# Attention shifts through one row matmul, the closing norm of a row tile spread over two pairs, and score banks for the Fourier stage's transposes and mapping

## The chip, the cores and the metric

The kernel runs on one core of a Trainium2 chip. The metric is device time in microseconds (us) for one execution, and lower is better. The kernel before takes 3379.32 us, the median of three runs (3378.93 to 3382.05).

## What is computed

One layer of an encoder over 4096 tokens and 16 prepended meta tokens, width 1024. The reference, cut to what matters:

```python
u = rmsnorm(h, norm_g)
f_in, f_gate, q, k, v, a_gate = split(u @ w_in)
f_out = (real(fftn(f_in, axes=(position, channel of its group))) @ w_fmix + b_fmix) * silu(f_gate)
q, k  = rope(rmsnorm(q, q_g)), rope(rmsnorm(k, k_g))     # 8 query heads, 2 kv heads of dim 64
a_out = softmax(q @ k.T * 64 ** -0.5) @ v * silu(a_gate)   # 4112 keys, no mask
h = rmsnorm(h + concat(f_out, a_out) @ w_out, final_g)
return h[:, 16:]
```

## The kernel before

Products are made in float16 with a high and a low part of an operand, three matmuls for one product. Phase A (to about 738 us in the trace) makes the projections and folds the input for the Fourier transform; q, k, v and both gates go to DRAM. Phase B does the Fourier transform's second half and the attention. The order of the work in phase B is written out by hand: each engine takes its instructions in the order in which the Python code issues them, SyncE (SP) issues all of phase B's DMAs in one queue, and an instruction that waits holds everything behind it on its engine.

**Pairs and steps.** Attention runs over 8 blocks of 512 queries, and in each over 4 pairs of heads: 32 pairs, numbered `i` from 0, `(b, p)` in the code. A pair has 66 steps `j`, 33 key tiles for each of its two heads. A step (`qk`, `pvm`) makes the scores of 512 queries against 128 keys in a score bank (L983, L984), has ScalarE (ACT) take the exponential into `pe` (L987), has GpSimd (POOL) or VectorE (DVE) make `rr`, the low part (L989), and four steps later multiplies both parts with V (L1004 to L1011). `on_dve` says which steps' `rr` DVE makes: two steps after each entry of the list `AT`. When a head's 33 tiles are done, ACT copies its accumulator (`tt`, L1015), DVE takes a reciprocal (L1017), and POOL makes four operations of it (`ob`, L1019 to L1022).

**Banks.** PSUM's eight banks are: two tiles of two banks each that are called `m`, two score banks `s`, one for the attention accumulator `o`, one for `pd`/`po`. A tile is taken in turn, and its next user waits for the last reader.

**The shift.** The exponential is taken of score minus the row's maximum, and the maximum must be known before the pair begins. So while pair `i` runs, `max_units(i+1)` makes the next pair's scores a first time in `m` tiles (L928, two groups at each entry of `AT`, 32 in all) and DVE takes their maxima (L929, `mx`). `meta` does so for the 16 meta tokens, 8 small matmuls for a pair (L936, L938). At step 58 `red` reduces and scales them (L943, L944, `nm`), at step 61 `fin` turns them with 8 matmuls (L951) into rows, and two ACT copies (L954) put these into rows 64 to 95 of `qB`. There they meet a constant 256 in K's second half, so that the second score matmul (L984) subtracts the shift.

**The output.** From block 1 on each pair also finishes one 128-row tile of the block before: `out_tr` at step `TR` = 8 turns 1024 mixed channels with eight transposes into an `m` tile (L1047), ACT and DVE split it (`mh` L1050, `ml` L1051), and 48 matmuls (L1064) at steps 13 to 36 and 41 to 64 make the output projection. `out_end` at step 2 of the next pair closes the tile: the sum of squares on ACT (L1079), eleven DVE operations of which ten are on 128x1 values (the root), and the scaling `yo` (L1083).

**The Fourier stage.** 18 units of 50 matmuls (L772, L775), each followed by `gather` (ACT), `trans` (four transposes into an `m` tile, L798, then `thl` on ACT, DVE and POOL) and `mix` (24 matmuls into an `m` tile, then `mo` on DVE, L838, and POOL, L840). `flist` holds them in order, and `f_step(n, heavy)` does up to `n` matmuls and `heavy` of the transposes or mappings. Before pair 0, where nothing but pair 0's maxima can run beside it (the start below), each round does two groups of maxima and `f_step(18, 1)`. In pairs 0 to 3 each step does `f_step(5, ...)`; then `wo_load` and `wo_prep` fetch and split the eight pieces of the output weights (L911, L915, L916) until step 258 of 264.

## Time and profile before

| | us |
|---|---|
| median of 3 runs | 3379.32 |
| profiled execution, its own time | 3381.74 |
| its span, first to last instruction | 3380.0 |
| PE busy (share of the span) | 3275.9 (97%) |
| DVE busy | 2369.8 (70%) |
| ACT busy | 1735.4 (51%) |
| POOL busy | 2223.6 (66%) |
| phase A, to the first unit's last Fourier matmul | 738 |
| start of phase B, to pair 0's first score | 85 |
| pairs 0 to 3 | 356 |
| pairs 4 to 31 and the tail | 2201 |

A matmul's recorded duration is longer than the time by which the next one can start, so a busy PE can still have short waits in it: the start-to-start distance of neighbours says how long a matmul holds the array. The execution's own time is 1.7 us more than its span.

### The profile page before, as it was taken

How to read it: one execution, taken by the hardware profiler on the slowest of the kernel's cores; microseconds unless marked ns; L12 is line 12 of the kernel's file. 1: busy time of each engine (PE TensorE's matmuls, PEld its weight loads, DVE VectorE, ACT ScalarE, POOL GpSimd, SP SyncE). 2: the span in 40 equal slices, each digit the busy share in tenths (PEclk: the TensorE clock that was granted, in tenths of full speed). 3: DMA queues.
4: the chain of work that ended last, by engine and by line, in shares of the span. 5: the costliest groups of instructions: out<-in, count | busy, mean ns of one | idle time of the engine just before them, and what ended most of it. 6: DMA issues, size and time to landing. Idle time of an engine off the chain costs nothing.

```text
span 3380.0 us, 79039 instructions
## 1 busy us (share of the span) xinstructions
PE 3275.9 (97%) x33333; PEld 1909.7 (56%) x33333; DVE 2369.8 (70%) x3250; ACT 1735.4 (51%) x3019; POOL 2223.6 (66%) x2131
## 2 busy tenths in 40 slices
PE   7999999988999999999999999999999999999998
PEld 4555555546666555555555555555555555555554
DVE  6766565537667877777777777777777777777764
ACT  5443443322555655555555555555555555555553
POOL 3655555323667877777777777777777777777762
PEclk9999999999999999999999999999999999999999
DMA  7444443437431120010001000100100010010001
GB/s 218 140 162 137 144 145 125 128 116 215 136 117 50 51 54 24 20 45 20 20 20 45 20 20 27 57 20 20 45 20 20 20 45 20 20 39 20 20 20 57
DMA packets 142330, 223.61 MB, mean 66 GB/s; under 512 B 30390, under 2 KB 85510, under 8 KB 137622
## 3 DMA queue, kind: packets, MB, share of 16 engines
q1 hardware_dynamic: 128150, 193.38, 18.5%
q10 hardware_dynamic: 13824, 25.17, 2.0%
q8 instruction: 261, 4.28, 0.5%
q14 instruction: 95, 0.78, 0.1%
HBM read 157.38 MB, written 61.14 MB: 65 GB/s over the span
## 4 chain that ended last, share of the span: by engine, by line
PE 67%; DVE 6%; issue 2%; ACT 1%; POOL 0%; ACTq 0%; POOLq 0%; DVEq 0%
PE s L983 12%; PE s L984 12%; PE o L1004 11%; PE po L1064 9%; PE m L928 7%; PE o L1011 7%; PE pd L775 2%; PE o L1009 2%; PE o L1007 2%; DVE mx L929 1%; DVE yo L1083 1%; PE m L1223 1%; PE m L1047 1%; DVE r1t L1097 1%; DVE rf L1098 1%
## 5 line engine op out<-in xcount | busy, mean ns | idle before, releaser
L989 POOL TENSOR_TENSOR rr<-pe 128x512 f16<-128x512 f32 (+1 forms) x1541 | 1634.4, 1075 | 629.5 <-ACT pe L987 623.8
L987 ACT ACTIVATE pe<-s 128x512 f32<-128x512 f32 (+1 forms) x2112 | 1259.4, 597 | 1038.6 <-PE s L984 1011.0
L929 DVE TENSOR_REDUCE mx<-m 128x2 f32<-128x1024 f32 x1024 | 1206.1, 1217 | 261.2 <-PE m L928 257.3
L1011 PE MATMUL o<-VV,rr 128*128 128x65 f16 x8448 | 974.7, 193 | 1.1 <-POOL rr L989 0.5
L1011 PEld LDWEIGHTS <-rr 128*128 128x128 f16 x8448 | 784.4, 98 | 186.3 <-issue 12.0
L1004 PE MATMUL o<-VV,pe 128*128 128x129 f16 x6336 | 842.1, 222 | 13.8 <-ACT tt L1015 10.9
L1004 PEld LDWEIGHTS <-pe 128*128 128x128 bf16 x6336 | 587.0, 97 | 390.5 <-issue 223.4
L983 PE MATMUL s<-qA,K 128*128 128x512 f16 (+1 forms) x2112 | 800.9, 379 | 0.7 <-ACT pe L987 0.7
L984 PE MATMUL s<-qB,K 128*128 128x512 f16 (+1 forms) x2112 | 800.6, 379 | 0.4 <-ACT qB L954 0.4
L989 DVE TENSOR_TENSOR rr<-pe 128x512 f16<-128x512 f32 x571 | 486.2, 852 | 222.9 <-ACT pe L987 219.9
L1007 PE MATMUL o<-VV,pe 128*128 128x65 f16 (+1 forms) x2112 | 411.0, 195 | 0.0
L1009 PE MATMUL o<-VV,pe 128*128 128x64 f16 (+1 forms) x2112 | 410.1, 194 | 0.0
L84 PE MATMUL ps<-wh,xh 128*128 128x512 f16 (+2 forms) x1032 | 366.0, 355 | 9.2 <-ACT xh L287 9.2
L85 PE MATMUL ps<-wl,xh 128*128 128x512 f16 (+2 forms) x1032 | 365.9, 355 | 4.7 <-DVE wl L270 4.7
L86 PE MATMUL ps<-wh,xl 128*128 128x512 f16 (+2 forms) x1032 | 366.1, 355 | 1.9 <-POOL xl L288 1.9
L928 PE MATMUL m<-K,qP 64*128 64x512 f16 x2048 | 320.4, 382 | 26.8 <-DMA bias<-bias 12.7
L928 PEld LDWEIGHTS <-qP 64*128 64x128 f16 x2048 | 66.3, 94 | 253.9 <-issue 246.0
L1009 PEld LDWEIGHTS <-pe 128*128 128x128 bf16 (+1 forms) x2112 | 208.7, 99 | 0.0
L983 PEld LDWEIGHTS <-K 128*128 128x128 f16 (+1 forms) x2112 | 202.9, 96 | 7.9 <-issue 1.1
L1007 PEld LDWEIGHTS <-pe 128*128 128x128 bf16 (+1 forms) x2112 | 206.2, 98 | 0.0
L984 PEld LDWEIGHTS <-K 128*128 128x128 f16 (+1 forms) x2112 | 204.7, 97 | 2.0 <-issue 1.9
L288 POOL TENSOR_TENSOR xl<-xt,xh 128x1024 f16<-128x1024 f32 (+1 forms) x33 | 68.7, 2082 | 155.6 <-ACT xh L287 155.5
(192 smaller groups left out, 3676.9 us busy)
## 6 DMA issues: line engine op xcount, KB each, us to landing
ct<-cd SPq DMA_DIRECT2D x16, 1088.0 KB
room<-x SPq DMA_DIRECT2D x32, 512.0 KB
xt<-xt SPq DMA_DIRECT2D x32, 512.0 KB
sg<-fx SPq DMA_DIRECT2D x16, 1024.0 KB
xr<-x SPq DMA_DIRECT2D x32, 512.0 KB
out<-yo SPq DMA_DIRECT2D x32, 512.0 KB
fg_d<-g ACTq DMA_DIRECT2D x32, 256.0 KB
ag_d<-g ACTq DMA_DIRECT2D x32, 256.0 KB
```

Of the source, the lines that this page charges most:

```text
L84: T.matmul(out, lh, rh, start=first, stop=False, skip_group_check=skip)
L86: T.matmul(out, ll, rh, start=False, stop=last, skip_group_check=skip)
L928: T.matmul(t[:, e], q[rs, s, p], K[kv][rs, 4 * c:4 * c + 4, 0], start=True, stop=True)
L929: V.tensor_reduce(mx[:, s, :, c], t, axis=AX.X, op=ALU.max)
L983: T.matmul(s[:n], K[kv][:, t, 0, :n], qa, start=True, stop=False)
L984: T.matmul(s[:n], K[kv][:, t, 1, :n], qb, start=False, stop=True)
L987: S.activation(pe[:n], s[:n], AF.Exp, scale=HD ** -0.5)
L989: eng.tensor_tensor(out=rr[:n], in0=pe[:n], in1=hi[:n], op=ALU.subtract)
L1004: T.matmul(o[:, c0:c0 + 129], hi[:n, cs], va, start=t == 0 and s == 0, stop=t == NT, skip_group_check=True)
L1007: T.matmul(o[:, c0:c0 + 65], hi[:n, cs], vh, start=False, stop=t == NT, skip_group_check=True)
L1009: T.matmul(o[:, c0:c0 + 64], hi[:n, cs], vl, start=False, stop=t == NT, skip_group_check=True)
L1011: T.matmul(o[:, c0:c0 + 65], rr[:n, cs], vh, start=False, stop=t == NT, skip_group_check=True)
```

## The change

It has five parts, beside an equal grouping of two DMAs (`runs`: the last six key tiles come with two loads instead of six).

1. **One row matmul.** `nm` becomes one 128x32 tile with the eight shifts of a row side by side. `fin`, now at step 63, is one matmul, and a new `put` at step 64, one DVE operation on 8 partitions with 1024 elements each, spreads the rows into `qB` through a mask cut from the identity. The 8 matmuls and both ACT copies go. K has eight rows of 256 in place of one. `red` moves to step 61.
2. **Meta once a block.** `meta` does all four pairs of a block at step `MT` = 60 of the pair before the block (32 small matmuls and two DVE operations); for block 0 it does two pairs at a time. The result is kept in `met`, already scaled, and `red` takes the minimum with it.
3. **The closing norm in steps.** `out_end` becomes `square` (ACT, step 62), `root` (ten DVE operations, step 65) and `scale` (`yo` and its DMA, step 13 of the next pair). `AT` has 16 entries and not 17, `TR` is 11, the output matmuls stand at steps 14 to 37 and 38 to 61, and `ml` is issued one step after its transposes.
4. **The start.** `trans` and `mix` take score banks instead of `m` tiles ahead of block 0; their DVE and POOL operations are held back (`behind`) and issued by `catch_up` after the next group of maxima. `qload(0)` and `fix_load` are issued ahead of `f_step(50, 0)`, `fix_prep` and the last key tiles after the first round; the last `f_step` does 25 matmuls and not 9.
5. **Block 0.** Each step does 3 Fourier matmuls and not 5, so that the last one stands at step 29 of pair 3 and not at step 38 of pair 2. `wo_prep` runs every fifth step from step 256 on, 6 of the 8 in pair 4, where the first output tile begins.

```diff
         for t in ksb:
             G.memset(t, 0.0)
-            G.memset(t[:, :, 1, 1, 0:1], 256.0)
+            G.memset(t[:, :, 1, 1, 0:8], 256.0)
...
-        def trans(u):
+        def trans(u, early):
             n, sk = (P, stk) if u < 16 else (64, stk8)
-            t = pm.tile([P, 2, 512], F32, tag="m", name="m")
-            ps = t[:, 0].rearrange("p (g c)->p g c", c=P)
+            if early:
+                ps = pq.tile([P, 512], F32, tag="s", name="s").rearrange("p (g c)->p g c", c=P)
+            else:
+                ps = pm.tile([P, 2, 512], F32, tag="m", name="m")[:, 0].rearrange("p (g c)->p g c", c=P)
...
             S.activation(th, ps[:, :, :n], AF.Copy)
-            V.tensor_tensor(out=tl, in0=ps[:, :, :n], in1=th, op=ALU.subtract)
             S.activation(thr, th[:, :, ::-1], AF.Copy)
-            G.tensor_copy(tlr, tl[:, :, ::-1])
+
+            def rest():
+                V.tensor_tensor(out=tl, in0=ps[:, :, :n], in1=th, op=ALU.subtract)
+                G.tensor_copy(tlr, tl[:, :, ::-1])
+
+            behind.append(rest)
...
             def red():
                 m = sm.tile([P, 4, 2], F32, tag="mm", name="mm")
                 V.tensor_reduce(m, mx, axis=AX.X, op=ALU.max)
-                V.tensor_scalar(out=n[:, :, :, 0], in0=m.rearrange("p s e->p e s"), scalar1=-1.0 / 256.0,
-                                scalar2=None, op0=ALU.mult)
+                V.scalar_tensor_tensor(out=n[:, 0:8].rearrange("p (e s)->p e s", s=4),
+                                       in0=m.rearrange("p s e->p e s"), scalar=-1.0 / 256.0,
+                                       in1=met[b][:, :, p], op0=ALU.mult, op1=ALU.min)
 
             def fin():
                 t = pm.tile([P, 2, 512], F32, tag="m", name="m")
-                for e in range(2):
-                    for s in range(4):
-                        T.matmul(t[64:96, e, s * P:(s + 1) * P], n[:, e, s], id16, start=s == 0, stop=True,
-                                 skip_group_check=s > 0)
-                for e in range(2):
-                    S.activation(qB[b % 2][64:96, :, 4 * e + p], t[64:96, e].rearrange("p (s c)->p s c", s=4),
-                                 AF.Copy)
+                T.matmul(t[64:96, 0, :P], n, id16, start=True, stop=True)
+                rowt.append(t)
+
+            def put():
+                t = rowt.pop()
+                V.tensor_tensor(
+                    out=qB[b % 2].rearrange("p s (e q) c->p e s q c", e=2)[64:72, :, :, p],
+                    in0=t[64:72, 0, :P].unsqueeze(1).unsqueeze(1).broadcast_to([8, 2, 4, P]),
+                    in1=id32[64:72, 64:72].rearrange("p (e s)->p e s", s=4).unsqueeze(3).broadcast_to([8, 2, 4, P]),
+                    op=ALU.mult)
...
-        AT = [0, 4, 8, 12, 15, 19, 22, 26, 29, 33, 36, 40, 43, 47, 50, 53, 56]
-        TR, O0, O1 = 8, 13, 41
+        AT = [0, 4, 8, 14, 18, 22, 26, 29, 33, 37, 41, 45, 48, 52, 55, 58]
+        MT, TR, O0, O1 = 60, 11, 14, 38
...
-            if g >= 6:
-                f_step(5, 1 if mid else 0)
+            catch_up()
+            if 6 <= g < 4 * 66:
+                f_step(3, 1 if mid else 0)
...
-                if j == 2 and prev:
-                    out_end(*prev)
-                    prev = None
+                if j == TR + 1 and b > 0:
+                    low()
+                if j == TR + 2 and prev:
+                    prev[2]()
+                if j == 62 and b > 0:
+                    prev = out_end(b - 1, p, halves[1])
+                    prev[0]()
+                if j == 65 and b > 0:
+                    prev[1]()
```

What ACT does from the end of one regular pair into the next (regular: a pair that also finishes an output tile). Before, from the shifts' two copies at step 61 on; `xr,ss` is the sum of squares, `tt` the head's accumulator, `mh` the output tile's high part:

```order
L954 ACTIVATE qB_7751<-m 32x4x128 x2
L987 ACTIVATE pe<-s 128x512 x3
L987 ACTIVATE pe<-s 16x512
L987 ACTIVATE pe<-s 128x512 x3
L1079 ACTIVATE xr,ss<-hh 128x1024
L987 ACTIVATE pe<-s 128x512
L1015 ACTIVATE tt<-o 128x452
L987 ACTIVATE pe<-s 128x512 x5
L1050 ACTIVATE mh<-m 128x1024
```

And now, from the sum of squares at step 62 on (ACT's exponentials are now at L1027, its other lines 40 to 42 further down than before):

```order
L1121 ACTIVATE xr,ss<-hh 128x1024
L1027 ACTIVATE pe<-s 128x512 x2
L1027 ACTIVATE pe<-s 16x512
L1027 ACTIVATE pe<-s 128x512 x4
L1055 ACTIVATE tt<-o 128x452
L1027 ACTIVATE pe<-s 128x512 x8
L1090 ACTIVATE mh<-m 128x1024
```

The copies into `qB` are gone, and the sum of squares stands four exponentials earlier, no longer between step 2's exponential and `tt`.

DVE in the same stretch, before, from the end of the root to the second key group after the transposes (`mx` are maxima of keys, `rc` the reciprocal):

```order
L1098 TENSOR_SCALAR rf<-r1t,rf 128x1
L1083 SCALAR_TENSOR_TENSOR yo<-hh,rf,fgb 128x1024
L1017 RECIPROCAL rc<-tt 128x4
L929 TENSOR_REDUCE mx<-m 128x2 x2
L989 TENSOR_TENSOR rr<-pe 128x512
L1051 TENSOR_TENSOR ml<-m,mh 128x1024
L929 TENSOR_REDUCE mx<-m 128x2
L989 TENSOR_TENSOR rr<-pe 128x512
```

And now, from the end of the root, which stands at step 65 of the pair before (the row ahead of its first one is `put`):

```order
L1146 TENSOR_SCALAR rf<-r1t,rf 128x1
L955 TENSOR_REDUCE mx<-m 128x2 x2
L1029 TENSOR_TENSOR rr<-pe 128x512
L1057 RECIPROCAL rc<-tt 128x4
L955 TENSOR_REDUCE mx<-m 128x2 x2
L1029 TENSOR_TENSOR rr<-pe 128x512
L955 TENSOR_REDUCE mx<-m 128x2 x2
L1029 TENSOR_TENSOR rr<-pe 128x512
L1092 TENSOR_TENSOR ml<-m,mh 128x1024
L1129 SCALAR_TENSOR_TENSOR yo<-hh,rf,fgb 128x1024
L955 TENSOR_REDUCE mx<-m 128x2 x2
```

The root has left the place between step 2's `rr` and step 4's maxima, and `yo` now comes after three pairs of maxima and `ml`.

SP's queue at the border of the phases, before (`k_d` is phase A's last store, `qP` the queries for pair 0's maxima, `ct` a unit's Fourier table, `fgu` a gate):

```order
L189 DMA k_d<-ko 128x512 x2
L828 DMA fgu<-fg_d 121x512
L828 DMA fgu<-fg_d 128x512
L105 DMA ct<-cd 128x4352
L707 DMA qP_7753<-q_d 64x4x512 x2
L744 DMA wst<-wst 128x1024
L745 DMA sgn<-sgn 128x2
L746 DMA bias<-bias 128x512
L118 DMA K_6590<-k_d 128x256 x6
```

And now:

```order
L189 DMA k_d<-ko 128x512 x2
L710 DMA qP_7753<-q_d 64x4x512 x2
L747 DMA wst<-wst 128x1024
L748 DMA sgn<-sgn 128x2
L749 DMA bias<-bias 128x512
L843 DMA fgu<-fg_d 121x512
L843 DMA fgu<-fg_d 128x512
L105 DMA ct<-cd 128x4352
```

`qP` and what `fix_prep` needs now stand ahead of the gate and the table.

## Prediction

> **What bounds the kernel now.** I read the page's engine shares first (PE 97%, no other over 70%), then the windows by stage. Columns: length, then busy time of PE, PEld, DVE, ACT and POOL, then PE's granted clock and DMA.

> ```profile
> 738.10:823.00 84.90, 59.36 (x544) 42.83 (x545) 53.88 (x56) 12.72 (x31) 19.90 (x15) 0.92 0.69 207
> 823.00:1104.90 281.90, 277.69 (x3246) 181.20 (x3246) 185.28 (x197) 146.00 (x271) 194.14 (x187) 0.99 0.35 108
> 1104.90:1178.90 74.00, 67.05 (x812) 38.39 (x810) 67.47 (x61) 46.92 (x78) 62.39 (x58) 1.00 0.16 51
> 1178.90:1254.30 75.40, 75.30 (x868) 42.92 (x866) 55.18 (x57) 42.37 (x72) 56.71 (x59) 1.00 0.17 43
> 1254.30:3256.40 2002.10, 1967.38 (x22418) 1118.98 (x22415) 1507.80 (x1768) 1125.20 (x1899) 1473.84 (x1483) 1.00 0.09 27
> ```

> These are the start, pairs 0 to 2, pair 3, pair 4, and pairs 5 to 30 (26 pairs of 77.0 us). PE is the bound in the pairs, with short holes; in the start it is idle for 25 of 85 us; in pair 3 DVE is busy for 67 of 74 us. Next the chain that ended last, at the seam of two regular pairs, and who PE waits for in pairs 5 to 30 (total, times, longest):

> ```profile
> 1954.10 1.50 DVE yo L1083
> 1955.70 1.12 DVE mx L929
> 1956.87 1.09 PE m L1047 x8
> PE m L1047 <- DVE mx L929: 21.3, 26, 0.8
> PE o L1004 <- ACT tt L1015: 9.9, 26, 0.4
> ```

> Once a pair the chain leaves PE: root and `yo` hold DVE, the maxima behind them are late, and the transposes of step 8 find no free `m` tile. That is 0.8 us of 77. The second hole, 0.4 us, is the wait for `tt`. Pair 4 is the control: it finishes an output tile, but no earlier tile's `out_end` falls into it, and it takes 75.4. So `out_end` in its old place costs 77.0 - 75.4 = 1.6 us a pair.

> **The seam (pairs 5 to 30).** `out_end` leaves step 2, so both holes go: -1.6 if nothing takes their place. *One row matmul:* eight take 0.62 us below, of which one alone lasts 0.22, so each further one costs (0.62 - 0.22)/7 = 0.057, and seven fewer are -0.4. *One event of maxima fewer:* the scores of steps 7 and 8 start 0.79 us apart, a bare step; a score matmul holds PE for 0.22. Into an event it takes 0.30 (1884.37 to 1884.67), and the event's four matmuls, which run in twos, take 0.54 and not 0.43: two changes of shape, -0.2.

> ```profile
> 1942.32 0.62 PE L951 MATMUL m<-id,nm 128*32 128x128 f16 x8
> L951 PE MATMUL m<-id,nm 128*32 128x128 f16 x216 | 16.7, 220 | 0.0
> 1877.72 0.38 PE L983 MATMUL s<-qA,K 128*128 128x512 f16 x1
> 1878.51 0.38 PE L983 MATMUL s<-qA,K 128*128 128x512 f16 x1
> 1884.15 0.38 PE L983 MATMUL s<-qA,K 128*128 128x512 f16 x1
> 1884.37 0.38 PE L984 MATMUL s<-qB,K 128*128 128x512 f16 x1
> 1884.67 0.60 PE L928 MATMUL m<-K,qP 64*128 64x512 f16 x4
> 1885.21 0.23 PE L1004 MATMUL o<-VV,pe 128*128 128x129 f16 x1
> ```

> *The other head's `tt`:* 52 heads end in these pairs and 26 waits are listed, so mid pair the wait stays under the view's limit of 0.15 us; now the maxima of step 37 stand there, -0.1. *Meta once a block:* the same 32 matmuls in one event of their own, at most +0.1 a pair. Sum so far -2.2.

> What comes in. (a) *The sum of squares at step 62.*

> ```profile
> 1873.19 0.60 ACT L987 ACTIVATE pe<-s 128x512 f32<-128x512 f32 x1 [0.19 <-PE s L984]
> 1873.69 1.05 ACT L1079 ACTIVATE xr<-hh 128x1024 f32<-128x1024 f32 x1
> 1874.73 0.59 ACT L987 ACTIVATE pe<-s 128x512 f32<-128x512 f32 x1
> 1874.86 0.15 DVE L1080 TENSOR_SCALAR ss<-ss 128x1 f32<-128x1 f32 x1 [0.19 <-ACT xr L1079]
> 1877.16 1.52 DVE L1083 SCALAR_TENSOR_TENSOR yo<-hh,rf,fgb 128x1024 f32<-128x1024 f32 x1
> ```

> It puts the next exponential 1.54 us behind the one ahead (1873.19 to 1874.73). There are two score banks, so step 65's scores wait for step 63's exponential. An exponential starts about 0.7 us after its step (two score matmuls and the hand-over), so step 63's ends 0.7 + 1.54 + 0.59 = 2.8 us after step 62's start. PE reaches step 65 after three bare steps and `fin`, 3 x 0.79 + 0.25 = 2.6: a new wait of 0.2 to 0.3. At step 2 the maxima of step 4 hid this; at 62 to 65 no output matmul and no maxima fill the steps. (b) *`put`.* Its nearest row is `ml`, also 1024 elements a partition from PSUM, 1.2 us:

> ```profile
> L1051 DVE TENSOR_TENSOR ml<-m,mh 128x1024 f16<-128x1024 f32 x26 | 31.8, 1224 | 1.3
> L929 DVE TENSOR_REDUCE mx<-m 128x2 f32<-128x1024 f32 x832 | 980.2, 1217 | 201.6 <-PE m L928 198.9
> L989 DVE TENSOR_TENSOR rr<-pe 128x512 f16<-128x512 f32 x442 | 371.0, 839 | 143.5 <-ACT pe L987 140.8
> ```

> The row matmul ends about 1.5 us after step 62's start, `put` at 2.8, and L984 of the next pair, its first reader, is due at 3.7: covered, with 0.9 us to spare. (c) *DVE from `put` to step 18:* `put` 1.2, root 2.3 (1874.86 to 1877.16), four pairs of maxima 9.7, four `rr` 3.4, `ml` 1.2, `yo` 1.5: 19.3 us. PE takes about 20.5 for it (20 steps of 0.79, five events at 0.6, eight transposes, five output matmuls). So DVE keeps up, by little, and each `m` tile is free just ahead of its user. (d) *POOL's four `ob` operations* at step 3 stand in front of step 4's `rr`.

> ```profile
> 1185.73 0.30 POOL L1021 TENSOR_TENSOR ob<-tt,ag 128x64 f32<-128x64 f32 x1
> 1186.68 8.92 POOL L989 TENSOR_TENSOR rr<-pe 128x512 f16<-128x512 f32 x8
> 1877.55 1.28 POOL L1021 TENSOR_TENSOR ob<-tt,ag 128x64 f32<-128x64 f32 x1
> ```

> In pair 4 that `rr` starts at 1186.68, 7.8 us after the pair (1178.90), and ends 8.92/8 = 1.1 later, at 8.9. Without transposes at step 8 PE wants it at 8 x 0.79 + 3 x 0.6 + 0.4 = 8.5; today the hole at step 8 covers it. I take +0.3, bounds 0 and 1.1 (one `rr`). Net -2.2 + 0.3 + 0.3 = -1.6 a pair, x 26 = -42 us; bounds -2.2 and -0.8 a pair (-57 and -21).

> The last three rows show one POOL operation at 0.30 beside maxima and at 1.28 beside `yo` (1877.16): the two engines delay each other. [...] It speaks against this change, which moves `yo` beside a row of waiting `rr`; rival B has the price.

> **The start.** Who PE waited for, the timeline, a window and a DMA size:

> ```profile
> PE m L928 <- DMA bias<-bias: 12.7, 1, 12.7
> PE m L928 <- DVE mo L838: 3.9, 5, 0.8
> PE m L951 <- DVE nm L944: 2.7, 1, 2.7
> PE m L928 <- DVE thl L801: 2.5, 5, 0.5
> PE m L798 <- issue: 2.5, 1, 2.5
> 738.55 1.28 SPq L707 DMA_DIRECT2D qP<-q_d  x2
> 750.00:755.00 5.00, 3.76 (x15) 1.73 (x16) 1.42 (x2) 0.40 (x1) 0.00 (x0) 0.50 0.61 136
> 752.78 2.82 PE L775 MATMUL pd<-acs,ct 128*128 128x264 f16 x12
> 767.84 1.51 PE L775 MATMUL pd<-acs,ct 128*128 128x264 f16 x12
> ct<-cd SPq DMA_DIRECT2D x16, 1088.0 KB
> ```

> The first maxima need `qP` (the first wait's label names a DMA of the same burst). It was issued at 738.55 behind a 1088 KB table and a gate of half that; at the start's 207 GB/s these are 8 us. With `qP` ahead I take 10 of the 12.7 (bounds 7 and 12.7). `fix_prep` still waits for its weights, now behind two maxima, and holds the third group's for about 3 us; the 2.5 us wait at the first transposes (L798) is the same wait in today's place, so nothing is counted. After the long wait the granted clock is 0.50, and twelve Fourier matmuls take 2.82 us against 1.51: 1.3 us more, of which I count none, since a wait of 3 us stays. [...]

> In the rounds, `trans` and `mix` no longer hold `m` tiles: 3.9 + 2.5 of waits, -6. `nm`'s 2.7 us go under 16 more matmuls (+1.7, taken from block 0). `put` in place of `fin`'s two copies: +0.5 to -0.5, 0. Sum -10 - 6 - 2.7 + 1.7 = -17; bounds -23 and -10 (if DVE, at 54 of 85 us, leads in the rounds and half the waits stay).

> **Block 0 and pair 4.** Pair 3 has no Fourier matmul and no output: pair 4's 75.4 less 48 output matmuls at 0.22 and transposes (1.1) is 64, and it took 74: 10 us of waiting for DVE, where `wo_prep` comes on top. Pairs 0 to 2 have 535 Fourier matmuls at 0.11 (1.51 us for twelve, less the overlap) and 12 units of 24 mapping matmuls at 0.057 and four transposes at 0.11: 80 us, and 3 x 64 = 192: 272 of 282, another 10. Spread at 3 a step, DVE has room (185 of 282 us). Of the 20 I leave 3 at pair 0's start and 4 where `wo_prep` now meets the first output tile, six of these in 28 steps:

> ```profile
> L916 DVE SCALAR_TENSOR_TENSOR wol<-wot,woh x8: 1225/1466/2014, 1096.7 to 1174.9; 128x1024 f16<-128x1024 f32 x8
> ```

> That is -13; the row matmul and the event, 0.6 in five pairs, -3; the 16 matmuls, -1.7. Sum -18; bounds -24 and -8 (`wo_prep` costs as much as today).

> **The end.** Pair 31's `tt` hole loses the sum of squares: -1.

> **Sum.** -42 - 17 - 18 - 1 = -78 us: the profiled execution from 3381.7 to 3304, the median of the runs, 2.4 below it, from 3379.3 to 3301.

> **Rivals.** *B: DVE and POOL become the bound at the seam.* `yo` shuts `rr` out for 1.5 us, DVE's 19.3 of 20.5 us turns into waits for `m` tiles, and half the seam's gain goes: 26 x 0.9 = +23, 3324. For it: the small margins in (c) and (d). Against: four steps between scores and their use. 0.2. *C: the start and block 0 give only their lower bounds* (-10, -8): +17, 3318. 0.08. *D: slower.* `red`, `fin`, `put`, L984 go from DVE to PE to DVE to PE within five steps at every seam. If `put` is over 0.9 us late, PE stands at step 0 with all scores behind it. The sum turns over where a seam loses 78/26 = 3.0 us more than forecast, `put` 3.9 late; at 4.5 us it is -78 + 117 = +39, 3418. Against: DVE has about 2 us of work in steps 59 to 63. 0.04. *E: no change,* 3379: every hole comes back as another. Against: pair 4 shows 75.4 without the hole. 0.02.

> **How the numbers follow.** The forecast has 0.66. All the bounds at once give -105 and -40; since they don't fall together I take 3276 to 3334, which holds B and C and leaves D, E and the ends out. A measurement of this kernel can tell about 0.2% (7 us) from no change: faster 0.94 (forecast, B, C), same 0.02 (E), slower 0.04 (D).

> **What would show it.** Right: the 26 pairs take 75.1 to 75.7 us; PE's waits at the transposes are gone, and one of 0.2 to 0.3 us for ACT stands at step 65; the start is 66 to 70 us, with the first maxima by 742; DVE is no longer in the chain in pair 3. B shows as waits for `rr` or of the maxima's matmuls at steps 4 to 18; C as DVE in the chain in pairs 3 and 4; D as a wait of the second score matmul for `put`. Wrong: pairs of 76.5 us or more.

## The result and the profile after

The changed kernel takes 3340.08 us, the median of four runs (3334.70 to 3343.77), against 3379.12 for the kernel before beside it; the ratio is 0.9881, with a 95% interval of 0.9864 to 0.9899. It is faster, as forecast, but by 39 us and not by 78, and 6 us above the upper end of the range. The profiled execution took 3343.77 us, the longest of the four, with a span of 3342.0. The interval is clear of 1, so the gain is real. That -39 is near the sum of all the prediction's lower bounds (-40) is chance: the seam gave its full forecast, and block 0 lies far outside its bounds.

The windows of the kernel after, by the prediction's stages: the start, pairs 0 to 2, pair 3, pair 4, pairs 5 to 30, and pair 31 with the tail. The columns are those of the prediction (length, busy PE, PEld, DVE, ACT, POOL, granted clock, DMA).

```profile
738.10:812.00 73.90, 58.63 (x545) 42.88 (x544) 54.27 (x59) 13.82 (x34) 18.50 (x15) 0.95 0.74 232
812.00:1088.00 276.00, 263.81 (x3064) 169.29 (x3064) 182.58 (x187) 135.81 (x249) 192.65 (x186) 0.99 0.32 99
1088.00:1174.20 86.20, 81.66 (x977) 46.76 (x975) 62.75 (x66) 45.12 (x81) 63.98 (x64) 0.98 0.12 42
1174.20:1256.00 81.80, 76.89 (x852) 43.21 (x849) 62.60 (x68) 46.95 (x78) 59.64 (x58) 0.98 0.27 82
1256.00:3215.20 1959.20, 1954.14 (x22221) 1103.49 (x22218) 1513.71 (x1755) 1093.51 (x1847) 1502.46 (x1509) 1.00 0.09 28
3215.20:3342.00 126.80, 112.38 (x1047) 65.42 (x1044) 62.65 (x132) 55.44 (x101) 45.04 (x45) 0.97 0.14 51
```

| stage, us | before | after | difference | forecast |
|---|---|---|---|---|
| start | 84.9 | 73.9 | -11 | -17 |
| pairs 0 to 4 | 431.3 | 444.0 | +12.7 | -18 |
| pairs 5 to 30 | 2002.1 | 1959.2 | -42.9 | -42 |
| pair 31 and tail | 123.6 | 126.8 | +3.2 | -1 |
| span | 3380.0 | 3342.0 | -38.0 | -78 |

The long stage came out to the microsecond: 75.35 us a pair, and the view of PE's waits has no row left for it. Most of what is missing lies in pairs 0 to 4, which were to get 18 us shorter and got 13 longer; the start gave 6 us less than forecast, and the end 4. PE's waits in pairs 0 to 4 of the kernel after (total, times, longest):

```profile
PE m L954 <- DVE mx L955: 9.3, 7, 1.3
PE o L1051 <- POOL rr L1029: 5.3, 5, 2.2
PE m L985 <- DVE nm L978: 3.9, 3, 1.7
PE m L954 <- DVE ml L1092: 2.2, 1, 2.2
PE s L1024 <- DVE qB L990: 1.6, 2, 1.0
```

With two rows below half a microsecond these are 23.0 us. One wait for `nm`, 1.4 us, ends at 811.90 and so ahead of pair 0's first score at 812.06; it belongs to the start, and 21.6 are left. The same view of the kernel before has 10.7 us for pairs 0 to 3 and no row for pair 4. So the waits explain 10.9 of the 12.7 us. The second cause is TensorE's clock. In pairs 0 to 4 of this profile it is granted at 0.50 for 13.7 us (6.8 from 812.86, 3.4 each from 1147.37 and 1195.15), in the kernel before for 3.4 (from 824.57). At 0.50 neighbouring score matmuls start 0.41 us apart (from 1147.37 on) and not 0.215, so about half of that time is lost, and this costs up to 5.1 us more than before; the last section has the windows ahead of these stretches. Together these are up to 16 us, so the work itself got up to 3 us shorter, for which the forecast had -3 (the row matmul and the event).

The first row is one mechanism, seven times. This is the first of them, the timeline of the kernel after around pair 0's step 29:

```profile
852.82 0.39 PE L954 MATMUL m<-K,qP 64*128 64x512 f16 x2
853.25 1.23 DVE L955 TENSOR_REDUCE mx<-m 128x2 f32<-128x1024 f32 x1 [0.61 <-PE m L954]
854.53 0.39 PE L954 MATMUL m<-K,qP 64*128 64x512 f16 x2 [1.32 <-DVE mx L955]
854.96 1.23 DVE L955 TENSOR_REDUCE mx<-m 128x2 f32<-128x1024 f32 x1 [0.48 <-PE m L954]
```

The transposes of a Fourier unit were issued at step 28 into an `m` tile. Its last reader, DVE's `thl`, is held back by `behind`, and `catch_up` issues it in step 29 behind that step's two key groups. DVE is idle for 0.61 us ahead of 853.25 and could have read the tile; instead both groups must share the other tile, and the second one waits until the first one's maximum is done. That happens wherever a transpose or mapping lies in the step ahead of an event, which the new table allows where two events stand three steps apart (26 and 29, 45 and 48, 52 and 55, 55 and 58). The old table has such places too, but in the kernel before the reader was issued together with its transposes.

### The profile page after: what moved, and what is told of

The parts are those of the page before. It is cut to its first block, busy times and chain, and to the rows that moved or that the text cites. A ratio compares the mean times of both kernels' runs of the same rounds, so it can differ in the third digit from the quotient of the medians.

```text
span 3342.0 us, 78621 instructions
## 1 busy us (share of the span) xinstructions
PE 3266.4 (98%) x33109; PEld 1889.9 (57%) x33109; DVE 2370.9 (71%) x3237; ACT 1696.5 (51%) x2955; POOL 2256.6 (68%) x2162
## 4 chain that ended last, share of the span: by engine, by line
PE 86%; POOL 5%; DVE 4%; ACT 2%; DMA 2%; issue 1%; SPq 0%; ACTq 0%; POOLq 0%; DVEq 0%
PE s L1023 13%; PE s L1024 12%; PE o L1044 11%; PE po L1104 9%; PE o L1051 7%; PE m L954 7%; PE ps L84 5%; PE ps L86 5%; PE ps L85 5%; POOL rr L1029 2%; PE pd L778 2%; PE o L1049 2%; PE o L1047 2%; DVE mx L955 1%; PE m L1286 1%
## 5 line engine op out<-in xcount | busy, mean ns | idle before, releaser
L1029 POOL TENSOR_TENSOR rr<-pe 128x512 f16<-128x512 f32 x1572 | 1696.0, 1095 | 594.1 <-ACT pe L1027 585.2
L1027 ACT ACTIVATE pe<-s 128x512 f32<-128x512 f32 (+1 forms) x2112 | 1256.4, 596 | 1098.0 <-PE s L1024 1011.3
L1051 PE MATMUL o<-VV,rr 128*128 128x65 f16 x8448 | 976.9, 193 | 10.4 <-POOL rr L1029 6.2
L1051 PEld LDWEIGHTS <-rr 128*128 128x128 f16 x8448 | 783.5, 98 | 179.3 <-POOL rr L1029 24.7
L1044 PE MATMUL o<-VV,pe 128*128 128x129 f16 x6336 | 850.9, 222 | 0.5 <-ACT tt L1055 0.5
L1029 DVE TENSOR_TENSOR rr<-pe 128x512 f16<-128x512 f32 x540 | 425.2, 788 | 226.3 <-ACT pe L1027 226.0
L1047 PE MATMUL o<-VV,pe 128*128 128x65 f16 (+1 forms) x2112 | 411.2, 195 | 0.0
L954 PE MATMUL m<-K,qP 64*128 64x512 f16 x2048 | 313.9, 383 | 18.9 <-DVE mx L955 16.7
L1047 PEld LDWEIGHTS <-pe 128*128 128x128 bf16 (+1 forms) x2112 | 206.4, 98 | 0.0
## 6 DMA issues: line engine op xcount, KB each, us to landing
ct<-cd SPq DMA_DIRECT2D x16, 1088.0 KB
```

The costliest lines, as they stand in the source:

```text
L954: T.matmul(t[:, e], q[rs, s, p], K[kv][rs, 4 * c:4 * c + 4, 0], start=True, stop=True)
L1027: S.activation(pe[:n], s[:n], AF.Exp, scale=HD ** -0.5)
L1029: eng.tensor_tensor(out=rr[:n], in0=pe[:n], in1=hi[:n], op=ALU.subtract)
L1044: T.matmul(o[:, c0:c0 + 129], hi[:n, cs], va, start=t == 0 and s == 0, stop=t == NT, skip_group_check=True)
L1047: T.matmul(o[:, c0:c0 + 65], hi[:n, cs], vh, start=False, stop=t == NT, skip_group_check=True)
L1051: T.matmul(o[:, c0:c0 + 65], rr[:n, cs], vh, start=False, stop=t == NT, skip_group_check=True)
```

## The experiments: block 0

**The held-back readers first.** (Label `readers_first`; as in all runs below, the edit is to the changed kernel unless another is named.)

```diff
+                catch_up()
                 for f in gs[:n]:
                     f()
```

> The changed kernel with the held-back readers of the DFT's transposes and mapping issued ahead of the next step's key maxima in place of behind them (nothing else moved). Theory: a reader that is held back keeps one of the two m tiles over the next step's maxima, so where two events stand three steps apart the second group waits for the first one's maximum; seven such waits of 1.49 us go, pairs 0 to 4 fall from 444 to 433-436 us and the median by 8 to 10. Rival: DVE's work sets pairs 0 to 2 anyhow, so that the waits only move to other places; pairs 0 to 4 stay within 3 us of 444.

Measured: 3329.72 us (3326.43 to 3332.01), ratio to before 0.9847 (0.9833 to 0.9862). Pairs 0 to 4 take 431.4 us, 12.6 less. PE's waits of this run in pairs 0 to 2:

```profile
PE s L1024 <- DVE qB L990: 1.0, 1, 1.0
PE m L954 <- DVE thl L815: 0.7, 3, 0.3
PE o L1051 <- POOL rr L1029: 0.7, 1, 0.7
```

The row of 9.3 us is gone and 0.7 us stand in its place. The theory holds, the rival falls: seven starts that were 1.49 us late each are 10.4 of the 12.6 us, and by 10.4 the median fell too. The other 2.2 go with the clock and not with the order: it is at 0.50 for 6.8 us of pairs 0 to 4 in this profile and for 13.7 in the changed kernel's. Pair 3 shows it: it has the same waits in both (4.5 and 4.6 us) and takes 84.8 us here and 86.2 there, and it takes 84.8 in `ml_at_once` too, where nothing of pair 3 differs from the changed kernel. One line of order in the code gives back some 10 of the 12.7 us by which pairs 0 to 4 had grown.

**`wo_prep` earlier.** Four Fourier steps in a step, `wo_prep` from pair 3's step 28 to 63.

```diff
-        W0 = 256
+        W0 = 226
...
-                f_step(3, 1 if mid else 0)
+                f_step(4, 1 if mid else 0)
```

> The changed kernel with four Fourier steps instead of three in each step of block 0, and wo_prep from pair 3's step 28 to 63 in place of pair 3's step 58 to pair 4's step 27. Theory: wo_prep at the seam and beside the first output tile makes the waits for nm and put there (1.9 and 0.8 us), for ml (2.4) and for the rr of steps 8 and 9 (2.1), and the slow matmuls behind them; pair 4 falls from 81.9 to 75.5-77 us, pairs 0 to 4 by 5 to 9 us. Rival: the work has to go somewhere, and at four a step DVE waits grow in pairs 0 to 3 by what pair 4 gains; pairs 0 to 4 stay within 3 us of 444.

Measured: 3333.29 us (3329.89 to 3337.01). Pair 4 falls from 81.8 to 75.7, pairs 0 to 4 to 438.1, 5.9 less; five waits for the shared tile remain. The theory's sum is met, but the rival has a part: pair 2 takes 97.5 us (92.7), and pair 3, at 83.6, now waits for maxima at steps 33 to 58. What `wo_prep` costs at the seam is to be seen on DVE in the kernel after; first pair 3's end, then pair 4's steps 12 to 14:

```profile
1170.99 0.82 DVE L978 SCALAR_TENSOR_TENSOR nm<-mm,met 128x8 f16<-128x8 f32 x1
1171.84 2.03 DVE L940 SCALAR_TENSOR_TENSOR wol<-wot,woh 128x1024 f16<-128x1024 f32 x1
1173.90 1.22 DVE L990 TENSOR_TENSOR qB<-m,id 8x1024 f16<-8x1024 f32 x1
```

```profile
1192.19 1.38 DVE L940 SCALAR_TENSOR_TENSOR wol<-wot,woh 128x1024 f16<-128x1024 f32 x1 [2.60 <-ACT woh L939]
1193.49 1.21 DVE L1092 TENSOR_TENSOR ml<-m,mh 128x1024 f16<-128x1024 f32 x1
```

`wol` stands between the shift's `nm` and `put`; and ahead of `ml`, where DVE is idle for 2.60 us because `wol` waits for ACT's `woh`, while PE waits for the tile that `ml` would free.

**No mapping at step 35.**

```diff
-                f_step(3, 1 if mid else 0)
+                f_step(5 if 36 <= g % 66 < 48 else 3, 1 if mid else 0)
...
-                    block0(66 * i + j, j - 2 in AT)
+                    block0(66 * i + j, j - 2 in AT and j != 35)
```

> The changed kernel without trans or mix at step 35 of block 0's pairs, and with five Fourier steps instead of three at steps 36 to 47, so that the pipeline doesn't fall behind. Theory: a mapping dealt at step 35 has its POOL multiplication (2.35 us) right ahead of the first head's four ob operations, and the two together make the rr of steps 38 to 41 late: the waits at steps 41 and 42 (0.2, 0.8 and 2.4 us, and about 0.8 of slow matmuls behind the longest) go, 4 us of 444; the seven waits for the shared tile stay or move by one or two. Rival: the ob operations and the row of POOL rr are enough by themselves; waits of the same size for rr stay at steps 41 and 42.

Measured: 3334.85 us (3333.04 to 3336.93), pairs 0 to 4 437.5, 6.5 less. POOL in the kernel after, ahead of the longest of the waits for `rr`:

```profile
1141.30 2.35 POOL L862 TENSOR_TENSOR mo<-mo,fgu 64x1024 f32<-64x1024 f32 x1
1143.61 0.97 POOL L1059 TENSOR_TENSOR ob<-tt 128x192 f32<-128x192 f32 x1
1144.66 0.59 POOL L1060 TENSOR_TENSOR ob<-ob,ag 128x192 f32<-128x192 f32 x1
...
1146.15 2.04 POOL L1029 TENSOR_TENSOR rr<-pe 128x512 f16<-128x512 f32 x2
```

An `rr` that PE wants at 1145 starts at 1146.15, 4.85 us after `mo` began. By the view of waits the one at step 41 of pair 3 falls from 2.2 to 0.7 us, the one of pair 1 (0.65) goes, and another of 1.4 appears at step 34 of pair 3. The theory holds for the place; the run doesn't give its price cleanly, since the Fourier work moved with it, one of the seven shared-tile waits went as well, and the clock is at 0.50 for 6.8 us of pairs 0 to 4 and not for 13.7.

**The three together, and `wo_prep` spread thinner.** `readers_first` and `no_map_at_35`; one `wo_prep` each eight steps from pair 3's step 42, its DVE half two steps behind its ACT half.

```diff
-        W0 = 256
+        W0 = 240
...
-            d, r = divmod(g - W0, 5)
+            d, r = divmod(g - W0, 8)
             if 0 <= d < ND and r == 0:
                 wo_prep(d)
+            if 0 <= d < ND and r == 2:
+                wo_low(d)
```

> The changed kernel with four things in block 0: the held-back readers ahead of the next step's key maxima; no trans or mix at step 35 and five Fourier steps at steps 36 to 47; wo_prep one each eight steps from pair 3's step 42 to pair 4's step 32; its DVE half two steps behind its ACT half. Theory (the tile held over, POOL's mapping ahead of ob, and wo_prep packed at the seam are the three causes): pairs 0 to 4 fall from 444 to 420-425 us, the median to 3316-3322. Rival: DVE in pair 3 is short in any order; what the parts gain doesn't add up, pairs 0 to 4 stay at 430 or more, the median at 3326 or more.

Measured: 3326.75 us (3325.73 to 3327.03), pairs 0 to 4 427.0. That lies between the theory (420 to 425) and the rival (430 or more): the gains don't add up (12.6 + 6.5 + 5.9 would be 25, and 17 came). The window of 12 us from pair 3's step 47 on, where no Fourier work is left, says why:

```profile
1138.00:1150.00 12.00, 10.81 (x133) 6.14 (x130) 11.96 (x11) 7.40 (x13) 10.66 (x10) 1.00 0.17 55
```

DVE is busy for 11.96 of the 12.00 us. The seven maxima and three `rr` that touch this window take 11.8 us, and a `wol` of 2.0 comes on top: in that stretch the rival is right. Two rows of the same run's timeline, of POOL and of DVE, point to a second reason:

```profile
1122.84 5.47 POOL L1033 TENSOR_TENSOR rr<-pe 128x512 f16<-128x512 f32 x5
1126.07 3.27 DVE L1033 TENSOR_TENSOR rr<-pe 128x512 f16<-128x512 f32 x1 [0.17 <-ACT pe L1031]
```

An `rr` that DVE does in 0.7 us in most places (the median of this run) takes 3.27 beside a full row of POOL's `rr`. It is one place, and no run here shows what it costs.

## The experiments: the start and the end

**The readers behind both maxima of a round.**

```diff
             gs.pop(0)()
-            catch_up()
             if gs:
                 gs.pop(0)()
+            catch_up()
             f_step(18, 1, True)
```

> The changed kernel with the held-back readers of the start issued behind both key maxima of a round in place of between them. Theory: the wait of 1.4 us once a unit is DVE's own work: the round with a mapping gives it 3.7 us (two maxima of 1.2 and the two mapping results of 0.64) against 2.2 us of PE, as that round ends early at the gather; the order inside the round changes little, and the start goes from 73.9 to 71-73 us. Rival: the order alone makes the second group wait; the five waits go and the start is 66-68 us.

Measured: 3339.34 us (3336.32 to 3342.38). From the first Fourier matmul to the first score (phase A ahead of it ends up to 3 us earlier or later from run to run, so stages are compared) the start takes 82.0 us against 80.6 in the changed kernel. In the eight other profiles whose start is the changed kernel's as it stands it takes 76.9 to 82.2, so a difference of 2 us says nothing here. The rival, 6 to 8 us less, falls; the theory's own 1 to 3 us less did not come either. PE's longest waits in the start, of the changed kernel and then of this run:

```profile
PE m L954 <- DVE mx L955: 7.4, 5, 1.5
```

```profile
PE s L86 <- DVE thl L815: 6.0, 5, 2.7
PE m L954 <- DVE mx L955: 1.5, 5, 0.3
```

The wait changes its name, from the maxima to `thl`, and keeps its size.

**The first pair's shift filled with Fourier work.**

```diff
         catch_up()
+        f_step(14, 1, True)
         fin()
+        catch_up()
+        f_step(18, 1, True)
         put()
```

> The changed kernel with 14 more Fourier matmuls ahead of the first pair's row matmul and 18 behind it, ahead of put. Theory: the waits for nm (1.4 us) and for put (1.0), and the two to three us of matmuls at half speed that follow them in each run, are idle time that Fourier work of block 0 can fill; start and pairs 0 to 4 together fall by 4 to 6 us. Rival: block 0 has the same waits whatever Fourier work it is given, and the first scores wait for something else; together within 2 us of 517.9.

Measured: 3330.34 us (3329.73 to 3331.88). Start (from the first Fourier matmul) and pairs 0 to 4 together fall from 524.6 to 513.3 us, by 11.3: twice the theory's 4 to 6. The median falls by 9.7. The wait for `nm` (1.4) is gone, that for `put` falls from 1.0 to 0.3, and the slow matmuls behind them are gone. But the Fourier units also stand elsewhere against the table, and five shared-tile waits are left of seven; and the clock is at 0.50 for 3.4 us of pairs 0 to 4 and not for 13.7. The theory had counted neither.

**The end.** The last pair's second output half at step 41, its sum of squares at 65, its root behind the tail's first transposes.

```diff
-                    for k, o in ((0, O0), (1, O1)):
+                    for k, o in ((0, O0), (1, O1 + 3 * (i == 31))):
...
-                if j == 62 and b > 0:
+                if j == 62 + 3 * (i == 31) and b > 0:
...
-                if j == 65 and b > 0:
+                if j == 65 and 0 < b and i < 31:
...
+        prev[1]()
         prev[2]()
```

> The changed kernel with the last pair's second output half at step 41 again (38 in all others), its sum of squares at step 65 and its root behind the first transposes of the tail. Theory: the wait of the second half's first matmul for hh (1.4 us) and the wait for qB behind the root (1.2) go; pair 31 and the tail from 126.8 to 124-125 us. Rival: the tail is a chain of its own and waits for the last head anyway; it stays within 0.7 us of 126.8.

Measured: 3336.34 us (3335.67 to 3338.36); pair 31 and the tail 123.4 us, 3.4 less. The theory holds. The two waits at stake, in the kernel after:

```profile
PE po L1104 <- DVE hh L1109: 1.2, 1, 1.2
PE m L1286 <- DVE qB L1275: 1.0, 1, 1.0
```

## The experiments: the seam

The seam's sum was right, so its parts were tried one at a time; all numbers are the mean of pairs 5 to 30 in the profiled execution. The old event table is that of the kernel before, with the transposes at step 8.

| | event table | norm | row matmul | `ml` a step later | us a pair |
|---|---|---|---|---|---|
| before | old | step 2 | no | no | 77.00 |
| `row_alone` | old | step 2 | yes | no | 76.62 |
| `norm_alone` | old | in steps | no | no | 77.33 |
| `norm_and_row` | old | in steps | yes | no | 76.73 |
| `norm_and_ml` | old | in steps | no | yes | 76.37 |
| `old_table` | old | in steps | yes, meta too | yes | 75.58 |
| `norm_old_place` | new | step 2 | yes, meta too | yes | 77.06 |
| `ml_at_once` | new | in steps | yes, meta too | no | 75.35 |
| after | new | in steps | yes, meta too | yes | 75.35 |

**The row matmul alone,** in the kernel before:

```diff
-                for e in range(2):
-                    for s in range(4):
-                        T.matmul(t[64:96, e, s * P:(s + 1) * P], n[:, e, s], id16, start=s == 0, stop=True,
...
+                T.matmul(t[64:96, 0, :P], n, id16, start=True, stop=True)
...
-                last = {58: red, 61: fin}
+                last = {58: red, 61: fin, 62: put}
```

> The kernel before with another part alone: one row matmul and put on DVE in place of eight row matmuls and two ACT copies, in the old places (steps 61 and 62). Theory: seven matmuls of 0.057 fewer are 0.4 us a pair, put is covered; pairs 5 to 30 take 76.6, the median falls by 10 to 13. Rival: the seven small matmuls stood in time that PE waits anyway (for nm, for put's row, for ACT); pairs stay at 76.9 to 77.1 and the median falls by less than 4.

Measured: 3369.21 us (3366.85 to 3371.96), ratio 0.9971 (0.9960 to 0.9983); 76.62 us a pair, 0.39 less. The theory holds in its size, the rival falls.

**The norm alone,** in the kernel before:

```diff
-        TR, O0, O1 = 8, 13, 41
+        TR, O0, O1 = 8, 13, 38
...
-                if j == 2 and prev:
-                    out_end(*prev)
-                    prev = None
+                if j == TR + 2 and prev:
+                    prev[2]()
+                if j == 62 and b > 0:
+                    prev = out_end(b - 1, p, halves[1])
+                    prev[0]()
+                if j == 65 and b > 0:
+                    prev[1]()
...
```

> The kernel before with one part of the change alone: the closing norm in its three steps (sum of squares at step 62, root at 65, yo two steps behind the transposes of the next pair; the second half of the output product starts at step 38 for that), with eight row matmuls, the old events and the old block 0. Theory: out_end's old place is worth 1.6 us a pair and the sum of squares at 62 costs 0.2 to 0.3, so that pairs 5 to 30 fall from 77.0 to 75.6-75.8 us and the median by 30 to 37. Rival: the holes come from DVE's load at the seam whatever the place of yo; pairs stay at 76.5 or more and the median falls by less than 13.

Measured: 3390.04 us (3386.32 to 3394.73), ratio 1.0038 (1.0023 to 1.0052): slower, and 77.33 us a pair. My theory fell: moving the norm gains nothing by itself. PE's waits in pairs 5 to 30, to be read against the prediction's 21.3 and 9.9:

```profile
PE m L928 <- DVE mx L929: 28.3, 51, 0.7
PE s L983 <- ACT pe L987: 12.0, 25, 0.5
```

The hole of the maxima moved from the transposes to the event at step 15, and the sum of squares costs 0.46 us a pair at step 65. DVE's timeline of this run, pair 14 from step 6 on:

```profile
1952.54 0.72 DVE L989 TENSOR_TENSOR rr<-pe 128x512 f16<-128x512 f32 x1 [0.23 <-ACT pe L987]
1955.36 1.23 DVE L1051 TENSOR_TENSOR ml<-m,mh 128x1024 f16<-128x1024 f32 x1 [2.09 <-ACT mh L1050]
1956.50 1.22 DVE L929 TENSOR_REDUCE mx<-m 128x2 f32<-128x1024 f32 x1
...
1958.63 2.06 DVE L1089 SCALAR_TENSOR_TENSOR yo<-hh,rf,fgb 128x1024 f32<-128x1024 f32 x1
1960.61 2.34 DVE L929 TENSOR_REDUCE mx<-m 128x2 f32<-128x1024 f32 x2
```

DVE stands still for 2.09 us at `ml`, which waits for ACT's `mh`. Behind it in the queue are a maximum that could have been taken and `yo`; the event's maxima at 1960.61 come late by as much.

**The norm with `ml` a step later,** in the kernel before, beside the edit of `norm_alone`:

```diff
                 if j == TR and b > 0:
-                    out_tr(b - 1, p)
+                    low = out_tr(b - 1, p)
...
+                if j == TR + 1 and b > 0:
+                    low()
```

> The kernel before with the closing norm in steps (as in the run of the norm alone) and ml issued one step behind the transposes. Theory: in the run of the norm alone DVE stands 2.1 us at ml, since mh is not yet there, with the maximum and yo queued behind it, and the event at step 15 pays; with ml a step later the maximum goes ahead and the 1.6 us of the prediction appear: pairs 5 to 30 take 75.8-76.2 us (77.35 without), the median 3340 to 3352. Rival: ml's place does nothing, pairs stay at 77.0 or more.

Measured: 3367.24 us (3364.53 to 3369.51), 76.37 us a pair: 0.96 less than with the norm alone. The mechanism holds in part; I had given it 1.15 to 1.55, and the median is 15 us above the 3352 at which the theory ends. Against the kernel before the norm now gains 0.63 a pair and not 1.6: PE still waits 12.0 us for ACT's exponentials at step 65 (0.46 a pair) and 5.9 for maxima at step 15 (0.23). The same stretch of DVE:

```profile
1949.77 1.23 DVE L929 TENSOR_REDUCE mx<-m 128x2 f32<-128x1024 f32 x1 [1.36 <-PE m L928]
1950.91 1.22 DVE L1052 TENSOR_TENSOR ml<-m,mh 128x1024 f16<-128x1024 f32 x1
1952.13 0.71 DVE L989 TENSOR_TENSOR rr<-pe 128x512 f16<-128x512 f32 x1
1952.77 2.06 DVE L1089 SCALAR_TENSOR_TENSOR yo<-hh,rf,fgb 128x1024 f32<-128x1024 f32 x1
```

The maximum now goes first and DVE waits no more for `mh`.

**The norm with the row matmul,** in the kernel before (the edits of `norm_alone` and `row_alone`).

> The kernel before with the closing norm in steps and the row matmul with put, ml at the transposes as before. Theory: the row matmul gives its 0.4 us, and a part of the wait behind the sum of squares (0.65 at step 65, where ACT no longer has the two row copies): pairs 5 to 30 take 76.5-77.0 us. Rival: the row matmul is what lets the norm gain; 76.0 or less.

Measured: 3374.72 us (3371.22 to 3378.68), 76.73 us a pair, as the theory has it: 0.60 less than with the norm alone, 0.39 of it the row matmul's own price. The wait of PE for ACT's exponentials falls from 12.0 to 7.0 us in pairs 5 to 30, since the two row copies no longer stand in ACT's queue ahead of the sum of squares.

**The changed kernel with the old table.**

```diff
-        AT = [0, 4, 8, 14, 18, 22, 26, 29, 33, 37, 41, 45, 48, 52, 55, 58]
-        MT, TR, O0, O1 = 60, 11, 14, 38
+        AT = [0, 4, 8, 12, 15, 19, 22, 26, 29, 33, 36, 40, 43, 47, 50, 53, 56]
+        MT, TR, O0, O1 = 60, 8, 13, 38
...
                     halves = out_units(b - 1, p)
+                    n = 1
+                if j == AT[-1]:
+                    n = len(gs)
```

> The changed kernel with the events of the key maxima at the steps of the kernel before (12, 15, 19 and so on, one group beside the transposes at step 8, output from step 13); norm in steps, row matmul, meta once a block as changed. Theory after the run of the norm alone: in the old table the second event behind the transposes (15) finds DVE busy with ml and yo, so pairs take 77.3 less 0.4 for the row matmul, 76.7 to 77.0 us, and the median rises by 34 to 45. Rival: the norm in steps gains its 1.6 us once the row matmul and meta are as changed; pairs take 75.3 to 75.9.

Measured: 3348.15 us (3346.77 to 3352.59), 75.58 us a pair. Here the theory that I had formed after the norm alone falls, and its rival holds: the table is worth 0.23 us a pair once `ml`, the row matmul and meta are as changed (PE waits 4.4 us for maxima at step 15, 0.17 a pair, and nothing else is listed). The parts tried in the kernel before don't make up the rest: `norm_and_ml` less 0.39 for the row matmul would be 75.98, and this run has 75.58. The 0.40 between them belong to meta once a block, to the later places of `red`, `fin` and `put`, or to how the parts work together, which no run separates; the wait for ACT at step 65, 7.0 us in `norm_and_row`, is no longer listed here.

**The changed kernel with the norm in its old place.**

```diff
-                if j == TR + 2 and prev:
-                    prev[2]()
-                if j == 62 and b > 0:
-                    prev = out_end(b - 1, p, halves[1])
-                    prev[0]()
-                if j == 65 and b > 0:
-                    prev[1]()
+                if j == 2 and prev:
+                    for f in prev:
+                        f()
+                    prev = None
+                if j == 65 and b > 0:
+                    prev = out_end(b - 1, p, halves[1])
...
```

> The changed kernel with the closing norm whole at step 2 of the next pair again, as in the kernel before; event table, transposes at step 11, row matmul and block 0 as changed. The prediction's seam term (the old place costs 1.6 us a pair, the sum of squares at 62 costs 0.2 to 0.3): pairs 5 to 30 rise from 75.35 to 76.6-76.8 us, the median by 32 to 38. Rival, after the run of the norm alone: the room comes from the event table (events four steps apart from 4 to 26, transposes at 11), and the norm's place is worth little; pairs stay at 75.1 to 75.8. Between the two: 75.9 to 76.5, both have a share.

Measured: 3381.93 us (3377.62 to 3384.86), ratio 1.0004 (0.9994 to 1.0013), 77.06 us a pair, 1.71 more than the changed kernel, where the forecast's terms gave 1.3 to 1.4. The term holds and is larger. PE's waits in pairs 5 to 30, where the changed kernel has none:

```profile
PE m L954 <- DVE mx L955: 40.3, 52, 0.8
PE o L1044 <- ACT tt L1055: 10.3, 26, 0.7
```

In the kernel before the prediction lists 31.2 us of such waits, here they are 50.6. So what the other parts save goes into waits for the norm, and without the norm in steps they leave the kernel where it was.

**The changed kernel with `ml` right behind the transposes.**

```diff
             S.activation(mh, tv, AF.Copy)
             pst[b, s] = [mh, ml, xr]
-            return lambda: V.tensor_tensor(out=ml, in0=tv, in1=mh, op=ALU.subtract)
+            V.tensor_tensor(out=ml, in0=tv, in1=mh, op=ALU.subtract)
+            return lambda: None
```

> The changed kernel with ml issued right behind the transposes instead of one step later. Theory: DVE stands at ml for mh again, and rr of the steps behind it, yo and the event at step 14 are late: pairs 5 to 30 rise from 75.35 to 75.9-76.8 us, the median by 15 to 38. Rival: with the transposes at 11 and no event between 8 and 14 the changed table has the room for it; pairs stay at 75.3-75.6, the median within 7 of 3340.

Measured: 3337.55 us (3332.59 to 3339.42), 75.35 us a pair: no change, the rival holds. With the transposes at step 11 and the next event at 14, DVE can afford to stand at `ml`. So the new table and the later `ml` cure the same wait, and either is enough for most of it. In the runs that have neither, the norm's move costs time: 0.33 us a pair alone (77.33 against 77.00) and 0.11 with the row matmul (76.73 against 76.62). (Pair 4 falls from 81.8 to 77.8 in this run: `ml` is then issued ahead of the `wol` of step 12, and the wait of 2.2 us goes, with the 3.4 us at half clock behind it.)

## The experiments: one version

**All that was mended.** `block0_mended`, `end_mended`, `start_filled`, and `wo_prep` at pair 3's steps 38 and 49 and pair 4's 0, 5, 9, 15, 20 and 25.

> The mended block 0 with wo_prep at pair 3's steps 38 and 49 and pair 4's 0, 5, 9, 15, 20 and 25, the mended end (second output half of the last pair at 41, root in the tail), and 32 more Fourier and transpose matmuls around the first pair's row matmul. Theory: pairs 0 to 4 take 420 to 424 us (427 with the mended block 0), the start and its slow matmuls lose 4 to 6, the end 3.4; the median 3309 to 3316. Rival: DVE is short in pair 3's steps without Fourier work and gives back what wo_prep's places gain; 3319 or more.

Measured: 3319.41 us (3318.22 to 3320.50), ratio to before 0.9818 (0.9801 to 0.9834). Pairs 0 to 4 take 420.4 us and the end 123.4, both as expected; the start, with 32 Fourier matmuls and four transposes more, takes 83.8 from the first Fourier matmul, 3.1 more than in the changed kernel. The median is 3 above the range of the theory and just where the rival begins, since the start gives less than I took.

**The start's readers over two rounds,** in that version:

```diff
             gs.pop(0)()
-            catch_up()
+            kinds = [k for k, _ in flist[:19]]
+            if "gather" not in kinds[:18]:
+                catch_up()
```

> The run with all mended, with the start's held-back readers kept for one more round wherever the next round ends at a gather and is short. Theory: the wait of 1.5 us once a unit comes from DVE having two maxima and two mapping results against the short round's 2.2 us of PE; spread over two rounds it falls to a few tenths, and the start loses 4 to 7 us (median 3319 to 3312-3316). Rival: DVE has its sum of work in any order; the start stays within 2 us, as with the readers behind both maxima.

Measured: 3315.86 us (3313.82 to 3317.48), ratio 0.9810 (0.9795 to 0.9825); the start falls from 83.8 to 79.3, by 4.5. PE's waits in the start, the row of the maxima before this edit and with it:

```profile
PE m L958 <- DVE mx L959: 7.6, 5, 1.5
```

```profile
PE m L958 <- DVE mx L959: 1.3, 4, 0.3
```

The theory holds: the round with a mapping has four DVE operations and ends early, and it helps to leave the mapping's two to the next round. The length of the start alone would not show it, since it differs by 5 us between profiles with the same start; the row of waits, shorter by 6.3, does. By the medians this version is 24 us faster than the changed kernel and 65 faster than the kernel before.

## Why the forecast was right on the seam and wrong on block 0

**The bound.** PE with short holes in the pairs: right. In pairs 5 to 30 PE is now busy for 1954.1 of 1959.2 us.

**The seam (-42 forecast, -42.9 measured).** The term for the norm's old place holds in the changed kernel (1.71 by putting it back), the one for the row matmul by itself (0.39 against 0.4). The waits of (a) and (d) are there in a regular pair, one smaller and one larger than the 0.3 each: by the distances of neighbouring matmuls in pair 5, 0.13 us at step 65 and 0.5 at steps 8 and 9, none of them in the view of waits. But the working left a part of the change without a price. In (c) I added up what DVE has to do from `put` to step 18, 19.3 us of 20.5, and called that covered. A sum doesn't see an engine that stands at the head of its queue: in the old order DVE loses 2.1 us at `ml` with work behind it, and then the norm's move is worth nothing (+0.3 us a pair). `ml` one step later, or the transposes at step 11, is what lets the norm's move pay, and the prediction spoke of neither as a condition. Nor do its terms add: without the norm in steps the other parts give nothing (77.06 against 77.00) where they were to give some 0.6, the step from `norm_and_ml` and the row matmul to `old_table` brings 0.40 where meta was counted as a loss of up to 0.1, and the norm 1.71 and not 1.3 to 1.4. The forecast came out because the change has all the parts; that the total fits to 1 us is in part luck.

**Rival B** was not seen: no wait for `rr` or of a maximum's matmul is listed in pairs 5 to 30. The waits for `rr` at steps 8 and 9 are there, as term (d), but at 0.5 us a pair and not at the 0.9 more that B took. And `yo` held no `rr` for the 1.5 us of B: in the trace of the kernel after one POOL `rr` beside `yo` takes 2.02 us in each of pairs 5 to 30, where the median of all is 1.04, so 1.0 us is what it loses.

**The start (-17 forecast; -11 by the prediction's window, 1.0 of which is phase A that ended earlier).** The wait for `qP` went as a whole, more than the 10 us of the term; 2.4 us for `fix_prep`'s weights are left, where the prediction left some 3, and 2.2 for the table `ct` are new. What failed is "in the rounds, `trans` and `mix` no longer hold `m` tiles: 3.9 + 2.5 of waits, -6": the tiles came free and 7.4 us of the same waits stayed, because DVE had to do the two mapping results between two maxima in a round that ends early. `start_readers_last` and `start_order` show it. The bound let half of these waits stay; all of them did. "`nm`'s 2.7 us go" and "`put`: 0" failed by 1.4 and 1.0 us. The 16 matmuls that were to fill the wait for `nm` are 5 in the trace, 350 Fourier matmuls ahead of pair 0 against 345, since the last `f_step` may do 25 and stops at its unit's gather.

**Block 0 and pair 4 (-18 forecast, +12.7 measured): the step that failed.** It is "Spread at 3 a step, DVE has room", with the 20 us of waiting ahead of it. Both tens were remainders: the length of a stretch less an estimate of PE's work. For pair 3 the view of waits has 6.7 us. PE's waits in pairs 0 to 2, in the kernel before, by the same view:

```profile
PE m L928 <- DVE mx L929: 1.5, 2, 0.8
PE m L951 <- DVE nm L944: 1.3, 1, 1.3
PE s L983 <- ACT pe L987: 0.5, 1, 0.5
```

With three rows of 0.4 us or less they are 4.1 us. So some 10 us were there to be had and not 20, and I let 13 go. (The count of 535 is wrong too, without effect: the trace has 555 Fourier matmuls in these pairs and 11 mapped units, not 12.) And the lower bound left out a loss: the change holds readers back in block 0 too, though the prediction priced this only for the start. That cost 10.4 us, the largest single loss. In place of 13 us of waits gone, 10.9 came on top. The clock was not in this sum at all, and half clock behind the new waits cost up to 5.1. The 4 us left for `wo_prep` at the first output tile were about right: `put`, `ml` and pair 3's `nm` make 4.5 us of waits there. The waits for `rr` by a mapping ahead of `ob` were not foreseen. I don't know an order that gives the 18: with all mended pairs 0 to 4 take 420.4 us, 10.9 less than before, and 4.5 of these are only moved, the 37 Fourier matmuls and four transposes that the start then has more (at 0.11). So block 0 and pair 4 are some 6 us better than before.

**Rival C** had the right place, DVE and POOL in the chain of pairs 3 and 4, but as a smaller gain; it was a loss. **D** and **E** were not seen: PE waits for `put` only where `wol` stands ahead of it, and in pair 0.

**The end (-1 forecast, +3.2 measured).** The second output half directly behind the first was not priced: in the last pair, where DVE makes two thirds of the `rr`, `hh` is late for it. `end_mended` takes 3.4 back.

## What to carry to other kernels

Add up an engine's work for a stretch, and then walk its queue in order: an instruction that waits with work behind it (here `ml`, for 2.09 us) costs what no sum shows, and an edit elsewhere may pay only once that instruction is moved. Whoever postpones a reader must look who takes the buffer's turn in the meantime; here one line of order was 10 us. A remainder (length less estimated work) is not a wait; ask the trace who waited before promising that it goes. And compare the granted clock of two profiles before putting their difference down to an edit.
